# Reciprocal roots of mean squares: one power operation on GpSimd in place of ten VectorE operations

## The chip, the cores and the metric

The kernel runs on one core of one Trainium2 chip. The metric is the device time of one execution in microseconds (us); the kernel before has a median of 2822.03 us over three runs, from 2821.3 to 2822.34. The engines are named as in the profile: PE is TensorE (matmuls and transposes; PEld its weight loads), DVE is VectorE, ACT is ScalarE, POOL is GpSimd, SP is SyncE, which issues nearly all DMAs.

## What is computed

One inference step of a two-layer decoder trunk for 1024 prompt tokens (with 16 meta tokens ahead of them) and 8 sequences of 8 sampled tokens. Layer 0 is a Mamba-2 mixer and a SwiGLU feed-forward; its output gives one shared K and V; layer 1 is sliding-window attention over them and a second feed-forward; a final norm ends it. Every norm divides by the root of a mean square:

```python
def _rmsnorm(x, g):
    xf = x.astype(jnp.float32)
    r = lax.rsqrt(jnp.mean(xf * xf, axis=-1, keepdims=True) + EPS)
    return (xf * r).astype(x.dtype) * g

def _gated_group_rmsnorm(y, z, g):
    u = (y * jax.nn.silu(z)).astype(jnp.float32).reshape(b, l, SSM_GROUPS, D_INNER // SSM_GROUPS)
    u = u * lax.rsqrt(jnp.mean(u * u, axis=-1, keepdims=True) + EPS)
    return u.reshape(b, l, D_INNER).astype(y.dtype) * g
```

Only `lax.rsqrt` is touched: one number for each token and norm (for each token and group in the gated norm).

## The kernel before

The tokens are worked on in two halves, of 592 and 512 (`HALVES`), and each half in blocks of up to 128 tokens. Activations stand with features on the 128 partitions and tokens along the free axis, as residual tiles `hA`, `big` or `hN`. A large product is a row of matmuls by 128 x 128 blocks of weights, three for each block: value and weight are split into a high and a low part (`uH`, `uL`, `wH`, `wL`), and three of the four products are taken (lines 75 to 77 and 1555 to 1557).

The mean squares of a block are columns: one number for each token, tokens on the partitions, and one column for each block of the half. So the function `rsqrt` (line 85) always works on a tile of 128 partitions and 1 to 5 columns. It is called 21 times, from four places:

- `input_half` (line 382), five times. ACT squares the rows of a block and sums them into `xv` (line 379), line 381 divides and adds EPS, and line 401 multiplies the rows by the root into `xn`. PE transposes `xn` (line 406), and ACT and DVE split the result into `uH` and `uL` (lines 81 and 82). Three calls stand at the start of the program, two near 500 us, while the mixer of the first half still runs.
- `norm` (line 820), eight times: the gated norm of each of four groups in each half. PE sums the squares with a column of ones (line 818), line 819 writes `gv`, line 824 puts the roots on a diagonal, PE spreads it over the partitions with a matmul (line 829), and line 832 multiplies. POOL sets `gv` to one first (line 816).
- `row_scale` (line 1145), six times: the norms ahead of the feed-forwards and of K, V and the queries. `col_scale` (lines 1158 and 1159) spreads the root in the same way, or ACT multiplies by it when it reads a product (line 2035).
- `Final.scale` (line 1825), twice. `turn` transposes the result on PE (line 1835) and multiplies by the root into `Y` (line 1843), which is written out.

The ten operations take the root by a shift and subtraction on the bits and two steps of refinement. Each reads what the one ahead of it wrote.

Other names that the text below uses: `gate_tile` (lines 776 and 777) makes the gate `zT` from an accumulator in PSUM by a tanh on ACT and an operation on DVE; `apply_gate` (line 783) multiplies it into `xT`, ACT squares the result (lines 786 and 789), and POOL adds up the squares (line 790). `Weights` loads weights (line 116), casts the high part on ACT (line 152) and takes the low part `wL` on DVE and on POOL in turn (line 158). `gb` is the gain of the first norm, loaded in line 358.

The order on each engine is not written by hand: the program is handed to a scheduler, which orders every engine's instructions by a timeline that it works out when the kernel is built. Each engine then runs its list in order, and an instruction that waits holds up all behind it on its engine.

Of the kernel before, what the change touches and what calls it, by code (L numbers as in the profile page):

```python
# [11 lines left out]
F32 = mybir.dt.float32  # L12
F32R = mybir.dt.float32r
I32 = mybir.dt.int32
AF = mybir.ActivationFunctionType
ALU = mybir.AluOpType
# [68 lines left out]
def rsqrt(nc, pool, v, n, tag):  # L85

    p = v.shape[0]
    si = pool.tile([128, n], I32, name="rs_i", tag="rs_i")
    y = pool.tile([128, n], F32, name=tag + "_y", tag=tag + "_y")
    t = pool.tile([128, n], F32, name="rs_t", tag="rs_t")  # L90
    nc.vector.tensor_scalar(si[:p], v.bitcast(I32), 1, None, ALU.logical_shift_right)
    nc.vector.tensor_scalar(si[:p], si[:p], -1, 0x5F3759DF, ALU.mult, ALU.add)
    nc.vector.tensor_tensor(t[:p], si[:p].bitcast(F32), si[:p].bitcast(F32), ALU.mult)
    nc.vector.scalar_tensor_tensor(t[:p], t[:p], -0.5, v, ALU.mult, ALU.mult)
    nc.vector.scalar_tensor_tensor(y[:p], t[:p], 1.5, si[:p].bitcast(F32), ALU.add, ALU.mult)
    nc.vector.tensor_tensor(t[:p], y[:p], y[:p], ALU.mult)
    nc.vector.tensor_tensor(t[:p], t[:p], v, ALU.mult)
    nc.vector.tensor_scalar(y[:p], y[:p], 0.375, None, ALU.mult)
    nc.vector.scalar_tensor_tensor(t[:p], t[:p], -10.0 / 3.0, t[:p], ALU.add, ALU.mult)
    nc.vector.scalar_tensor_tensor(y[:p], t[:p], 5.0, y[:p], ALU.add, ALU.mult)  # L100
    return y


# [168 lines left out]
class Mamba:  # L272
# [61 lines left out]
    def input_half(self, hf):  # L334
# [35 lines left out]
        for cs in groups:  # L370
# [9 lines left out]
            w = v[:nr, : len(cs)]  # L380
            nc.vector.tensor_scalar(w, w, 1.0 / D, EPS, ALU.mult, ALU.add)
            r = rsqrt(nc, self.wk, w, len(cs), f"rx{cs[0]}")
            self.rtok += [r[:, i : i + 1] for i in range(len(cs))]
            if hf:
# [425 lines left out]
    def norm(self, G, g):  # L810
# [6 lines left out]
        for c, (o, m) in enumerate(H["blocks"]):  # L817
            nc.tensor.matmul(ps[:m, 2 * c : 2 * c + 1], G.ssq[:, o : o + m], K.ones[:, 0:1], start=True, stop=True)
            nc.vector.tensor_scalar(v[:m, c : c + 1], ps[:m, 2 * c : 2 * c + 1], 0.25 / 512, EPS, ALU.mult, ALU.add)
        r = rsqrt(nc, self.wk, v[:, :nb], nb, "rg")  # L820

        dg = lambda o, m: G.ssq[:m, o : o + m]
# [305 lines left out]
def row_scale(K, blocks, pool, ps, apart=None):  # L1128


    nc = K.nc
    nb = len(blocks)
    v = pool.tile([128, nb], F32, name="rv", tag=f"rv{nb}")
    nc.gpsimd.memset(v[:], 1.0)
    for i, (o, n) in enumerate(blocks):
        parts = [K.tot[:, o : o + n]] + ([] if apart is None else [apart[:, o - blocks[0][0] : o - blocks[0][0] + n]])
        for x, src in enumerate(parts):
            nc.tensor.matmul(ps[:n, 2 * i : 2 * i + 1], src, K.ones[:, 0:1], start=x == 0, stop=x == len(parts) - 1)
    pv = ps[:, : 2 * nb].rearrange("p (i two) -> p i two", two=2)[:, :, 0]
    f = 0 if blocks[0][1] == 128 else 1  # L1140
    if f:
        n0 = blocks[0][1]
        nc.vector.tensor_scalar(v[:n0, 0:1], pv[:n0, 0:1], 1.0 / D, EPS, ALU.mult, ALU.add)
    nc.vector.tensor_scalar(v[:, f:], pv[:, f:], 1.0 / D, EPS, ALU.mult, ALU.add)
    return rsqrt(nc, pool, v[:], nb, f"rr{nb}")
# [1468 lines left out]
```

## Time and profile before

| | |
|---|---|
| median of three runs | 2822.03 us |
| span of the profiled execution | 2818.3 us |
| median less span | 3.7 us |
| PE idle in the span | 82.2 us |
| mean granted clock of PE | 0.992 |
| operations in the function, all calls | 210 on DVE |

The profile gives the profiled execution by its span, from the first instruction to the last; the 3.7 us beside it are what the median of the runs has around that. In rows of the timeline the first column is the start in us from the beginning of the span and the second the duration in us, and square brackets give the idle time of that engine just ahead of the row and what ended it. In rows of groups the number behind "x" counts instructions, the next ones are busy us and mean ns of one, and behind the second bar stands the idle time ahead of them. In rows of waits stand the waiting engine, tile and line, whom it waited for, the us in total, the times, and the longest. Rows of windows give, for a stretch, its length, the busy us of PE, PEld, DVE, ACT and POOL with counts, the granted clock of PE (1.00 is full), the DMA share and GB/s.

### The profile page before, as it was taken

To read this page: it belongs to the slowest core of one execution; us is meant where nothing else is said; L and a number is where in the kernel's file an instruction comes from. 1 tells how busy PE (TensorE), PEld (TensorE's weight loads), DVE (VectorE), ACT (ScalarE), POOL (GpSimd) and SP (SyncE) were. 2 spreads that over 40 slices of the span, in tenths; PEclk is the share of its full clock that TensorE was granted. 3 is DMA by queue.
4 is the path that set the end of the run, shared out by engine and by line. 5 is a ranking of instruction groups with operands and counts; after the bars stand their busy time and mean duration, and the time that the engine had idled before them with its cause. 6 is when DMAs were issued, how large, how long until landed. Compare 5 with 4: busy or idle time off the path is not lost. (4 is left out here: it accounts for less than half of the span.)

```text
span 2818.3 us, 51270 instructions
## 1 busy us (share of the span) xinstructions
PE 2736.1 (97%) x19990; PEld 2536.6 (90%) x19990; DVE 2023.9 (72%) x3649; ACT 1230.4 (44%) x2596; POOL 495.8 (18%) x692
## 2 busy tenths in 40 slices
PE   7999999899999899999999999999999999999998
PEld 7988999887888799999999997766999999999998
DVE  6779676647665698777779792455489777777886
ACT  4777554346542344333343233456344333434224
POOL 2566444314223100000000002343210000000000
PEclk9999999999999999999999999999999999999999
DMA  6776767465554524444468663001814443438754
GB/s 206 251 226 226 262 225 241 163 233 199 200 184 155 168 77 166 150 142 138 154 223 326 241 221 98 23 25 41 223 60 144 159 141 130 158 141 289 272 210 159
DMA packets 328289, 496.58 MB, mean 176 GB/s; under 512 B 24607, under 2 KB 222687, under 8 KB 328017
## 3 DMA queue, kind: packets, MB, share of 16 engines
q1 hardware_dynamic: 324590, 486.74, 51.3%
q10 hardware_dynamic: 3456, 6.56, 0.6%
q8 instruction: 158, 2.59, 0.4%
q14 instruction: 85, 0.70, 0.1%
HBM read 317.93 MB, written 175.30 MB: 175 GB/s over the span
## 5 line engine op out<-in xcount | busy, mean ns | idle before, releaser
L1211 ACT CAST wo<-ws 128x512 fp32r<-128x512 f32 x428 | 263.9, 620 | 531.5 <-PE wacc L1556 240.3
L1555 PE MATMUL dacc<-bo,wo 128*128 128x276 f32 (+1 forms) x1232 | 357.7, 291 | 3.7 <-DVE hN L1584 1.4
L1556 PE MATMUL dacc<-bo,wo 128*128 128x276 f32 (+1 forms) x1232 | 355.6, 289 | 0.0
L1557 PE MATMUL dacc<-bo,wo 128*128 128x276 f32 (+1 forms) x1232 | 355.5, 289 | 0.0
L1212 DVE TENSOR_TENSOR wo<-ws,wo 128x512 fp32r<-128x512 f32 x428 | 296.8, 698 | 52.3 <-ACT wo L1211 43.7
L75 PE MATMUL acc<-uH,wH 128*128 128x296 f32 (+1 forms) x840 | 277.6, 331 | 1.8 <-DVE th L777 1.0
L77 PE MATMUL acc<-uH,wL 128*128 128x296 f32 (+1 forms) x840 | 277.0, 330 | 0.4 <-POOL wL L158 0.4
L76 PE MATMUL acc<-uL,wH 128*128 128x296 f32 (+1 forms) x840 | 276.0, 329 | 0.0
L1555 PEld LDWEIGHTS dacc<-bo,wo 128*128 128x128 f32 x1232 | 231.9, 188 | 4.9 <-ACT sumX L1743 1.9
L1556 PEld LDWEIGHTS dacc<-bo,wo 128*128 128x128 f32 x1232 | 231.8, 188 | 0.0
L1557 PEld LDWEIGHTS dacc<-bo,wo 128*128 128x128 f32 x1232 | 231.7, 188 | 0.0
L75 PEld LDWEIGHTS acc<-uH,wH 128*128 128x128 f32 x840 | 159.5, 190 | 17.3 <-issue 6.3
L76 PEld LDWEIGHTS acc<-uL,wH 128*128 128x128 f32 x840 | 159.4, 190 | 12.4 <-issue 4.1
L77 PEld LDWEIGHTS acc<-uH,wL 128*128 128x128 f32 x840 | 159.4, 190 | 11.3 <-issue 2.2
L600 DVE SCALAR_TENSOR_TENSOR cc<-raw,convw,cc 128x616 f32<-128x616 f32 (+1 forms) x144 | 137.5, 958 | 38.7 <-ACT cc L598 36.8
L75 PE MATMUL acc<-yH,wH 128*128 128x296 f32 (+1 forms) x360 | 121.9, 339 | 9.8 <-DVE zT L777 5.9
L2408 POOL MEMSET mask<- 128x64 f32 x1 | 0.2, 151 | 720.3 <-PE dacc L1557 720.3
L77 PE MATMUL acc<-yH,wL 128*128 128x296 f32 (+1 forms) x360 | 119.7, 333 | 1.2 <-DMA wL<-kept 1.2
L76 PE MATMUL acc<-yL,wH 128*128 128x296 f32 (+1 forms) x360 | 120.0, 333 | 0.0
L1731 DVE TENSOR_TENSOR hN<-hN,dacc 128x552 f32<-128x552 f32 (+1 forms) x132 | 94.7, 723 | 20.7 <-PE dacc L1557 20.1
L1555 PE MATMUL wacc<-N4H,wo 128*128 128x276 f32 (+1 forms) x352 | 102.8, 292 | 4.4 <-DVE hA L1568 2.4
L1211 ACT CAST wo<-sum 128x512 fp32r<-128x512 f32 x62 | 38.5, 621 | 155.3 <-PE wacc L1556 107.2
(605 smaller groups left out, 8631.0 us busy)
## 6 DMA issues: line engine op xcount, KB each, us to landing
kept<-wH SPq DMA_DIRECT2D x56, 512.0 KB
kept<-wL SPq DMA_DIRECT2D x56, 512.0 KB
ws<-ffn_w_gate SPq DMA_DIRECT2D x44, 512.0 KB
ws<-ffn_w_up SPq DMA_DIRECT2D x44, 512.0 KB
ws<-ffn_w_down SPq DMA_DIRECT2D x44, 512.0 KB
ws<-ssm_w_in SPq DMA_DIRECT2D x40, 512.0 KB
wH<-kept SPq DMA_DIRECT2D x38, 512.0 KB
wL<-kept SPq DMA_DIRECT2D x38, 512.0 KB
```

The costliest lines, as they stand in the source:

```text
L75: nc.tensor.matmul(out, wH, xH, start=start, stop=False)
L76: nc.tensor.matmul(out, wH, xL, start=False, stop=False)
L77: nc.tensor.matmul(out, wL, xH, start=False, stop=stop)
L600: nc.vector.scalar_tensor_tensor(o, raw[:, k : k + n], w(k), o, ALU.mult, ALU.add)
L1211: nc.scalar.copy(H, src)
L1212: (low or nc.vector).tensor_tensor(L, src, H.bitcast(F32), ALU.subtract)
L1555: nc.tensor.matmul(out, wH, xH, start=start, stop=False, skip_group_check=True)
L1556: nc.tensor.matmul(out, wH, xL, start=False, stop=False, skip_group_check=True)
L1557: nc.tensor.matmul(out, wL, xH, start=False, stop=stop, skip_group_check=True)
L1731: add = lambda d, s: nc.vector.tensor_tensor(d, d, s, ALU.add)
L2408: nc.gpsimd.memset(A.mask0[:, :NS], NEG)
```

## The change

`rsqrt` fills a tile of up to five columns with -0.5 on POOL and raises the mean squares to that power in one two-input POOL operation. The ten DVE operations and the tiles `rs_i` and `rs_t` go.

```diff
 def rsqrt(nc, pool, v, n, tag):
 
     p = v.shape[0]
-    si = pool.tile([128, n], I32, name="rs_i", tag="rs_i")
+    e = pool.tile([128, 5], F32, name="rs_e", tag="rs_e")
     y = pool.tile([128, n], F32, name=tag + "_y", tag=tag + "_y")
-    t = pool.tile([128, n], F32, name="rs_t", tag="rs_t")
-    nc.vector.tensor_scalar(si[:p], v.bitcast(I32), 1, None, ALU.logical_shift_right)
-    nc.vector.tensor_scalar(si[:p], si[:p], -1, 0x5F3759DF, ALU.mult, ALU.add)
-    nc.vector.tensor_tensor(t[:p], si[:p].bitcast(F32), si[:p].bitcast(F32), ALU.mult)
-    nc.vector.scalar_tensor_tensor(t[:p], t[:p], -0.5, v, ALU.mult, ALU.mult)
-    nc.vector.scalar_tensor_tensor(y[:p], t[:p], 1.5, si[:p].bitcast(F32), ALU.add, ALU.mult)
-    nc.vector.tensor_tensor(t[:p], y[:p], y[:p], ALU.mult)
-    nc.vector.tensor_tensor(t[:p], t[:p], v, ALU.mult)
-    nc.vector.tensor_scalar(y[:p], y[:p], 0.375, None, ALU.mult)
-    nc.vector.scalar_tensor_tensor(t[:p], t[:p], -10.0 / 3.0, t[:p], ALU.add, ALU.mult)
-    nc.vector.scalar_tensor_tensor(y[:p], t[:p], 5.0, y[:p], ALU.add, ALU.mult)
+    nc.gpsimd.memset(e[:, :n], -0.5)
+    nc.gpsimd.tensor_tensor(y[:p], v, e[:p, :n], ALU.pow)
     return y
```

Behind the function every line number is smaller by nine in the changed kernel: 392 there is 401 before, 774 is 783, 768 is 777, 372 is 381. Since the scheduler orders the whole program anew, rows move at other places too, on all engines, most of them between 32 and 490 us.

At the start of the program, POOL's list in the changed kernel, from the first row behind its memsets to the first low parts of weights (`rx_y` is the root, `xv` the mean square, `rs_e` the tile of -0.5):

```order
L91 ISA
L91 TENSOR_TENSOR rx_y<-xv,rs_e 80x1
L90 MEMSET rs_e 128x2
L91 TENSOR_TENSOR rx_y<-xv,rs_e 128x2
L90 MEMSET rs_e 128x5
L91 TENSOR_TENSOR rx_y<-xv,rs_e 128x2
L90 MEMSET rs_e 128x5
L149 TENSOR_TENSOR wL<-ws,wH 128x512 x2
```

Before, the row `ISA` and the two rows of `wL` followed each other with nothing between; now three powers, each waiting for a mean square of DVE, stand ahead of these `wL`.

DVE's list at the second call of the start, before (the copy to `hA` moves transposed rows out of PSUM):

```order
L381 TENSOR_SCALAR xv<-xv 128x2
L91 TENSOR_SCALAR rs_i<-xv 128x2
L82 TENSOR_TENSOR uL_94<-ps,uH_92 128x4x80
L92 TENSOR_SCALAR rs_i<-rs_i 128x2
L82 TENSOR_TENSOR uL_95<-ps,uH_93 128x4x80
L93 TENSOR_TENSOR rs_t<-rs_i 128x2
L396 COPY hA<-ps 128x4x128
L94 SCALAR_TENSOR_TENSOR rs_t<-rs_t,xv 128x2
```

and in the changed kernel:

```order
L82 TENSOR_TENSOR uL_94<-ps,uH_92 128x4x80
L387 COPY hA<-ps 128x4x128
L372 TENSOR_SCALAR xv<-xv 128x2
L82 TENSOR_TENSOR uL_95<-ps,uH_93 128x4x80
L392 SCALAR_TENSOR_TENSOR xn<-xr,rx_y,gb 128x512 x2
L392 SCALAR_TENSOR_TENSOR xn<-tot,rx_y,gb 128x512 x2
L372 TENSOR_SCALAR xv<-xv 128x2
L149 TENSOR_TENSOR wL<-ws,wH 128x1024
```

The copy has moved ahead of the mean square, and the rows of `xn` follow with one other operation between.

DVE's list near 493 us, at the first call for the second half, before:

```order
L92 TENSOR_SCALAR rs_i<-rs_i 128x2
L783 TENSOR_TENSOR xT<-xT,zT 128x592 x3
L93 TENSOR_TENSOR rs_t<-rs_i 128x2
L94 SCALAR_TENSOR_TENSOR rs_t<-rs_t,xv 128x2
L95 SCALAR_TENSOR_TENSOR rx_y<-rs_t,rs_i 128x2
L96 TENSOR_TENSOR rs_t<-rx_y 128x2
L97 TENSOR_TENSOR rs_t<-rs_t,xv 128x2
L98 TENSOR_SCALAR rx_y<-rx_y 128x2
L99 SCALAR_TENSOR_TENSOR rs_t<-rs_t 128x2
L100 SCALAR_TENSOR_TENSOR rx_y<-rs_t,rx_y 128x2
L401 SCALAR_TENSOR_TENSOR xn<-xr,rx_y,gb 128x512 x4
L777 SCALAR_TENSOR_TENSOR zT<-zT,acc 128x592
```

and in the changed kernel:

```order
L688 TENSOR_TENSOR S<-S,ps 128x512
L372 TENSOR_SCALAR xv<-xv 128x2
L774 TENSOR_TENSOR xT<-xT,zT 128x592 x3
L392 SCALAR_TENSOR_TENSOR xn<-xr,rx_y,gb 128x512 x4
L768 SCALAR_TENSOR_TENSOR zT<-zT,acc 128x592
L843 TENSOR_TENSOR hA<-hA,acc 128x592
```

The eight rows of the function behind `xT` and the two ahead of it are gone, and `xn` stands right behind `xT`; the order of the others is the same. On POOL the power of this call stands between the rows `xT<-xT,tot` and `sq<-sq,th`.

## The prediction

> **What bounds the kernel now.** I read the page's head first, then the waits of TensorE, then the two stretches in which those waits lie.
>
> ```profile
> span 2818.3 us, 51270 instructions
> PE 2736.1 (97%) x19990; PEld 2536.6 (90%) x19990; DVE 2023.9 (72%) x3649; ACT 1230.4 (44%) x2596; POOL 495.8 (18%) x692
> ```
>
> TensorE (PE) is busy for 2736.1 of 2818.3 us. The matmuls stay, so a change off TensorE can win back at most the 82.2 us in which it is idle, plus what slow restarts cost. The span is that of the profiled execution; the median of the three runs, 2822.0 us, lies 3.7 us above it, and I apply every difference to that median.
>
> The waits of PE, and the row of one removed line:
>
> ```profile
> PE ps L406 <- DVE xn L401: 8.7, 3, 3.7
> PE acc L75 <- DVE zT L777: 6.6, 2, 5.9
> L92 DVE TENSOR_SCALAR rs_i<-rs_i x21: 149/171/536, 6.9 to 2806.2; 128x5 int32<-128x5 int32 x10, 128x4 int32<-128x4 int32 x6, 128x2 int32<-128x2 int32 x4, 80x1 int32<-80x1 int32 x1
> ```
>
> There are 21 calls of the function. Ten operations each at a median of about 0.17 us make 210 x 0.17 = 36 us of VectorE (DVE) work. Its engine is idle for 28% of the span, so this sum says nothing yet: what counts is where a result of the function ends a wait of PE. I followed all 21 calls; PE waits behind six of them: the three at the start, one at 499 us, one at 937 and the last.
>
> **The price of the new operation.** No row shows a power on GpSimd (POOL). The nearest rows and the hop between the engines:
>
> ```profile
> L1872 POOL TENSOR_TENSOR rt<-kr,rope_sb 128x32 f32<-128x32 f32 (+1 forms) x36 | 8.1, 256 | 35.6 <-ACT kr L2035 35.6
> 31.73 0.22 DVE L237 COPY gains<-ps 128x64 f32<-128x64 f32 x1 [1.10 <-PE ps L235]
> 32.04 0.62 POOL L1021 TENSOR_TENSOR wdt<-wdt,gains 128x256 f32<-128x256 f32 x1 [8.35 <-DVE gains L237]
> ```
>
> From below, a power takes no less than the shortest two-input POOL row, 0.26 us. From above, ten such operations for the ten steps give 2.6 us. That is no hard end, since a routine inside the engine may do more than ten steps; longer ones are a rival below. I take **d = 0.8 us**, the middle of 0.26 and 2.6 by ratio. The hop from DVE to POOL is 32.04 - 31.95 = 0.1 us, and I take the same back. A link from the mean square to its first reader then takes d + 0.2 = 1.0 us. The constant's memset is issued ahead of time and costs 0.1 us of an idle POOL.
>
> **The tail: 0.8 us.**
>
> ```profile
> 2805.99 0.17 DVE L91 TENSOR_SCALAR rs_i<-rv 128x5 int32<-128x5 int32 x1
> 2807.81 2.05 DVE L1843 TENSOR_SCALAR Y<-dacc,fr_y 128x512 f32<-128x512 f32 x3
> 2808.61 1.76 PE L1835 MATMUL dacc<-cmask_sb,hN 128*128 128x128 f32 x8 [1.88 <-DVE Y L1843]
> ```
>
> Here the chain is bare: PE waits for Y, Y for the root. The link is 2807.81 - 2805.99 = 1.82 us now and 1.0 after, and nothing else lies beside it until the end.
>
> **The last gated norm: 0.85 us.**
>
> ```profile
> 935.03 0.17 DVE L91 TENSOR_SCALAR rs_i<-gv 128x4 int32<-128x4 int32 x1
> 936.89 0.87 DVE L824 TENSOR_SCALAR sq<-cmask_sb,rg_y 128x128 f32<-128x128 f32 x4
> 937.23 0.49 PE L829 MATMUL acc<-sq,cmask_sb 128*128 128x128 f32 x2 [1.53 <-DVE sq L824]
> ```
>
> The link is 936.89 - 935.03 = 1.86 us now. It shrinks by about 0.85, less than the 1.53 us in which PE waits.
>
> **The start: 1.5 us.** All of the first 31 us feed the first large matmul.
>
> ```profile
> 6.70 0.15 DVE L91 TENSOR_SCALAR rs_i<-xv 80x1 int32<-80x1 int32 x1
> 9.54 1.41 DVE L401 SCALAR_TENSOR_TENSOR xn<-xr,rx_y,gb 80x512 f32<-80x512 f32 x2 [1.18 <-DMA gb<-ssm_norm_g]
> 13.53 0.49 DVE L82 TENSOR_TENSOR uL<-ps,uH 128x320 fp32r<-128x320 f32 x1
> 14.00 0.69 DVE L396 COPY hA<-ps 128x512 f32<-128x512 f32 x1
> 15.87 1.42 DVE L401 SCALAR_TENSOR_TENSOR xn<-xr,rx_y,gb 128x512 f32<-128x512 f32 x2
> 18.61 3.57 POOL L158 TENSOR_TENSOR wL<-ws,wH 128x512 fp32r<-128x512 f32 x2 [17.61 <-ACT wH L152]
> 19.73 1.23 DVE L93 TENSOR_TENSOR rs_t<-rs_i 128x2 f32<-128x2 f32 x1
> 25.62 2.74 DVE L401 SCALAR_TENSOR_TENSOR xn<-S,rx_y,gb 128x512 f32<-128x512 f32 x4
> 31.63 0.40 PE L75 MATMUL acc<-uH,wH 128*128 128x296 f32 x1
> ```
>
> The first call wins nothing: its reader waits for the DMA of gb until 9.54. In the second, the new DVE order puts the copy L396 where the second L82 now stands, so that it ends at 13.53 + 0.69 = 14.2, and the mean square behind it; 0.17 us for the square and a link of 1.0 let xn start at 15.4 instead of 15.87: 0.5 us. For the third, nine more small steps leave DVE between 15.7 and 25.6. Eight of them take 0.07 us (where they overlap) to 0.17 us each, and L93 takes 1.23: 1.8 to 2.6 us. Against that, xn of this group moves up beside POOL's two L158, and each may hold up one xn for 1.25 us: 2.5 us. The bounds are -0.2 and 3.1; I take the middle.
>
> **The wait at 499 us: 1.1 us, or 7.3.** This is the largest single wait behind a root.
>
> ```profile
> 493.16 0.43 DVE L381 TENSOR_SCALAR xv<-xv 128x2 f32<-128x2 f32 x1
> 493.90 2.14 DVE L783 TENSOR_TENSOR xT<-xT,zT 128x592 f32<-128x592 f32 x3
> 496.23 1.47 POOL L790 TENSOR_TENSOR sq<-sq,th 128x592 f32<-128x592 f32 x1 [2.67 <-ACT th L789]
> 496.34 1.38 DVE L95 SCALAR_TENSOR_TENSOR rx_y<-rs_t,rs_i 128x2 f32<-128x2 f32 x1
> 497.65 2.52 POOL L158 TENSOR_TENSOR wL<-ws,wH 128x512 fp32r<-128x512 f32 x2
> 497.75 1.21 DVE L96 TENSOR_TENSOR rs_t<-rx_y 128x2 f32<-128x2 f32 x1
> 501.61 0.16 DVE L100 SCALAR_TENSOR_TENSOR rx_y<-rs_t,rx_y 128x2 f32<-128x2 f32 x1
> 501.81 2.74 DVE L401 SCALAR_TENSOR_TENSOR xn<-xr,rx_y,gb 128x512 f32<-128x512 f32 x4
> 504.46 0.76 DVE L777 SCALAR_TENSOR_TENSOR zT<-zT,acc 128x592 f32<-128x592 f32 x1
> 505.28 0.61 PE L75 MATMUL acc<-yH,wH 128*128 128x296 f32 x1 [5.88 <-DVE zT L777]
> ```
>
> PE waits from 499.40 until L777 has read its accumulator. Steps on two columns, 0.16 us elsewhere, take 1.2 to 1.4 us here: L95 lasts as long as POOL's L790, and L96 ends with the first half of POOL's L158. So a DVE operation with two SBUF operands sits out the POOL operation under way. The engines take turns, and the function loses about 5 us to that.
>
> ```profile
> 505.28:508.20 2.92, 2.92 (x12) 2.92 (x13) 1.31 (x2) 0.70 (x1) 0.74 (x1) 0.50 0.00 0
> 511.00:514.00 3.00, 3.00 (x24) 3.00 (x23) 1.71 (x2) 0.66 (x2) 0.00 (x0) 1.00 0.58 238
> ```
>
> After the wait 12 matmuls take 2.92 us at a granted clock of 0.50, where 12 take 1.5 at 1.00: 1.4 us more. If xn ran undisturbed, xT would end at 495.8, xn at 498.6 and L777 at 499.3: the whole wait and the slow restart would go, 5.9 + 1.4 = 7.3 us. But xn has two SBUF operands as well, and it now moves beside the POOL work from which it was clear at 501.81. Taking turns with 0.71 us per xT, 0.8 for the power, 0.69 per xn, 1.47 for L790 and 1.26 for each half of L158: the power runs between two xT, xT ends at 496.6, three POOL operations slip between four xn, and L777 starts at 496.6 + 4 x 0.69 + 1.47 + 2 x 1.26 = 503.3 instead of 504.46. I take 1.1 us, by the rows of L95 and L96.
>
> The Trainium skill's GPSIMD Engine Reference, section Key points, says that POOL shares its SBUF interfaces with VectorE, in contention with instructions that have two SBUF inputs. The trace agrees by the 1.21 us of L96 against 0.16. By that rule the sum keeps 1.1 at this place; without it, it takes 7.3.
>
> **What hides the rest.** In both feed-forward norms PE reaches the reader by its own order, later than the root is there:
>
> ```profile
> 981.65 0.87 DVE L1158 TENSOR_SCALAR tot<-cmask_sb,rr_y 128x128 f32<-128x128 f32 x4
> 985.97 1.05 PE L1159 MATMUL ps<-tot,cmask_sb 128*128 128x128 f32 x8
> 2088.90 1.01 DVE L1158 TENSOR_SCALAR tot<-cmask_sb,rr_y 32x32 f32<-32x32 f32 x5
> ```
>
> At 981.65 + 0.87 the factor is ready 3.5 us ahead of PE; at 2088.90 it is ready 2 us ahead. A link that is 0.8 us shorter wins nothing there, and one 2 us longer costs nothing. The other calls have PE busy behind them as well. A wait of POOL in its own order is hardly new:
>
> ```profile
> L816 POOL MEMSET gv<- 128x8 f32 x8 | 0.8, 104 | 25.1 <-DVE rs_t L97 25.1
> ```
>
> This memset stands on POOL near the new power and now waits 25.1 us in all for step L97 of the function; the power waits for the earlier mean square. Queued behind it are the copies of raw and the product L737.
>
> **Sum**: 0.8 + 0.85 + 1.5 + 1.1 = 4.25 us, so 2822.0 - 4.25 = **2817.8 us**.
>
> The same page, section Engine selection, advises VectorE for elementwise work and gives GpSimd as 1.96 times slower. An estimate by that figure, twice the 0.17 us of a DVE step, makes a power of 0.33 us, and the sum about 6 us. No run here shows it for a power.
>
> **The rivals.**
> 1. *The mid wait goes wholly*: xn runs ahead of POOL. For it: DVE issues the four xn back to back. Against it: L95 to L99 each met a POOL operation. Price: 6.2 us more, 2811.6 us.
> 2. *The power is long.* Each microsecond of d adds one at the tail, at 937, at 499 and about one at the start, so the gain is gone at d = 0.8 + 4.25/4 = 1.9 us, and from 3.3 us the kernel is slower than a measurement can miss. For it: one operation does ten steps' work and more. Against it: the tiles have at most 5 columns. At d = 5: tail and 937 +3.4 each; the start +5 (first root at 6.7 + 5.2 = 11.9, past the 9.54 of gb, and the second behind it on POOL); 499 +3; 2088.9 overruns its 2 us by 1.4. That is 16 us: 2838.
> 3. *Another order.* The scheduler moves other work too between 32 and 490 us:
>
> ```profile
> 32.00:490.00 458.00, 446.53 (x3531) 412.95 (x3530) 332.79 (x526) 276.47 (x660) 231.67 (x268) 0.99 0.71 233
> ```
>
> PE is idle there for 458 - 446.5 = 11.5 us. That may double or halve: 2829 or 2812. I see no sign either way.
> 4. *POOL cannot start early.* Its first two-input operation in the trace is at 18.61; the new one is due at 6.8, and its cover ends at 9.54. Up to 18.6 + 0.8 + 0.1 - 9.5 = 10 us, if it is not ready before; the middle gives 2823. POOL has been idle since 1.0, which speaks against it. The same page, section Instruction dispatch, states about 6 us for the first call of a loaded kernel; from 1.0 that ends at 7 us, within the cover.
>
> **Chances.** Forecast 0.42, the mid wait gone 0.18, a long power 0.20, another order 0.14, a late start 0.06. A difference of 0.2%, 5.6 us, is about what a measurement of this kernel can tell from none. Below 2816.4 lie the second case, a third of the first and some of the order: 0.36. Above 2827.7 lie most of the long powers and some of the order: 0.24. The rest, 0.40, is no difference. The lower end takes every gain at its bound (3.1 + 7.3 + 1.4 + 1.4 at d = 0.26): 2808.8. At d = 2.6 the sum is 3 us of loss; the upper end is set at 2832, so that only the longer powers stay out. The forecast's own range is 2814 to 2822.
>
> **What would show it.** The power's row on POOL gives d. At the tail, the time from the last mean square to Y should be 1.0 us. At 935 PE's wait for L824 should be near 0.7. At 499 PE's wait for zT should be near 4.8 us with xn stretched beyond 0.75 each; if it is gone, the turns are wrong. The first large matmul should start near 30.1 instead of 31.63. The forecast is wrong if d is over 1.9 us, or if PE's waits between 32 and 490 us sum to much else than 11.5.

## The result, and the profile after

The changed kernel takes **2807.43 us** (median of 4 runs, 2804.66 to 2810.73); the kernel before took 2821.91 us in the same session (4 runs, 2821.3 to 2822.34). The ratio is **0.9946, 95% interval 0.9933 to 0.9960**: 14.5 us less, where 4.25 us were forecast. A later session gave 0.9939 (0.9927 to 0.9950). The profiled execution of the changed kernel took 2804.66 us, at the fast end of its four.

The head of the page, the main waits of TensorE and the power's groups (minimum, median and maximum in ns; first and last start in us):

```profile
span 2802.9 us, 51082 instructions
PE 2734.6 (98%) x19990; PEld 2536.4 (90%) x19990; DVE 1993.7 (71%) x3439; ACT 1229.3 (44%) x2596; POOL 518.6 (19%) x734
PE ps L397 <- DVE xn L392: 5.3, 3, 3.3
PE acc L75 <- DVE zT L768: 3.8, 2, 3.0
L91 POOL TENSOR_TENSOR rg_y<-gv,rs_e x8: 1004/1098/1575, 213.2 to 927.3; 128x5 f32<-128x5 f32 x4, 128x4 f32<-128x4 f32 x4
L91 POOL TENSOR_TENSOR rx_y<-xv,rs_e x5: 548/711/1603, 6.8 to 520.6; 128x2 f32<-128x2 f32 x4, 80x1 f32<-80x1 f32 x1
L91 POOL TENSOR_TENSOR fr_y<-rv,rs_e x2: 1167/1168/1168, 2767.9 to 2791.2; 128x5 f32<-128x5 f32 x2
```

PE's idle time falls from 82.2 to 68.3 us; its busy time falls by 1.5. So in this pair of profiles nearly the whole gain is waits that went. A power takes 0.55 us on one column, 0.71 on two and 1.0 to 1.2 on four or five, and up to 1.6 us where DVE works beside it.

The two bare links, at the last gated norm and in the tail, in the timeline:

```profile
927.32 1.02 POOL L91 TENSOR_TENSOR rg_y<-gv,rs_e 128x4 f32<-128x4 f32 x1 [15.66 <-DVE gv L810]
928.71 0.49 PE L820 MATMUL acc<-sq,cmask_sb 128*128 128x128 f32 x2 [0.77 <-DVE sq L815]
2790.88 0.14 DVE L1815 TENSOR_SCALAR rv<-dacc 32x1 f32<-32x1 f32 x1
2791.16 1.17 POOL L91 TENSOR_TENSOR fr_y<-rv,rs_e 128x5 f32<-128x5 f32 x1 [21.97 <-DVE rv L1815]
2792.36 2.06 DVE L1834 TENSOR_SCALAR Y<-dacc,fr_y 128x512 f32<-128x512 f32 x3 [1.35 <-POOL fr_y L91]
```

PE's wait at the gated norm is 0.77 us instead of 1.53. In the tail DVE waits 1.35 us for the root; the steps there took 1.82 us.

The place that was the wait of 5.88 us at 505 us:

```profile
489.54 0.43 DVE L372 TENSOR_SCALAR xv<-xv 128x2 f32<-128x2 f32 x1
489.98 2.15 DVE L774 TENSOR_TENSOR xT<-xT,zT 128x592 f32<-128x592 f32 x3
490.05 1.27 POOL L91 TENSOR_TENSOR rx_y<-xv,rs_e 128x2 f32<-128x2 f32 x1
492.05 6.01 DVE L392 SCALAR_TENSOR_TENSOR xn<-xr,rx_y,gb 128x512 f32<-128x512 f32 x4
492.32 1.82 POOL L781 TENSOR_TENSOR sq<-sq,th 128x592 f32<-128x592 f32 x1 [0.84 <-ACT th L780]
494.09 3.41 POOL L149 TENSOR_TENSOR wL<-ws,wH 128x512 fp32r<-128x512 f32 x2
497.98 0.76 DVE L768 SCALAR_TENSOR_TENSOR zT<-zT,acc 128x592 f32<-128x592 f32 x1
498.79 0.62 PE L75 MATMUL acc<-yH,wH 128*128 128x296 f32 x1 [3.00 <-DVE zT L768]
```

Four `xn` that took 2.74 us before now take 6.01, 1.5 us each, beside three POOL operations, and PE still waits 3.00 us. The turns came, as forecast; the wait shrank by 2.9 us all the same.

### Where the time went

All profiles hold 19990 matmuls, so the start of the n-th can be compared between them. (At 262 us the n-th is not the same operation in every kernel, since the scheduler moves rows there: that cut is rough.) The table cuts the program at matmuls 263, 1854, 3612, 3862, 5997, 6513, 18091 and the last, counted from 0; the times are those of the first profile of the kernel before. Each entry is how much longer a stretch took than in that profile, averaged over profiles of kernels "without" the power in the calls that count for the stretch (the first profile itself as 0) and "with" it:

- Up to 490 us the three calls of the start decide: without are both profiles of the kernel before, `e2_rg`, `e3_rr`, `e6_late` and `e9_b_one`; with are both of the changed kernel, `e1_rx`, `e4_dead`, `e5_start` and `e10_a_one`.
- From 490 to 534 us the two late calls decide: without are both of the kernel before, `e2_rg`, `e3_rr` and `e5_start`; with are both of the changed kernel, `e1_rx` and `e6_late` (`e4_dead`, left out here, has -1.6).
- Behind 534 us, without are both of the kernel before, `e1_rx`, `e5_start`, `e6_late` and `e9_b_one`; with are both of the changed kernel, `e4_dead` and `e10_a_one`.

| stretch, us | forecast | without (profiles) | with (profiles) | difference |
|---|---|---|---|---|
| 0 to 52, the start | -1.5 | 0.15 (6) | -2.06 (6) | -2.2 |
| 52 to 262 | 0 | -0.10 (6) | -2.76 (6) | -2.7, rough |
| 262 to 490 | 0 | 0.45 (6) | 0.65 (6) | 0.2, rough |
| 490 to 534 | -1.1 | -0.32 (5) | -4.80 (4) | **-4.5** |
| 534 to 927 | 0 | 0.05 (6) | 0.24 (4) | 0.2 |
| 927 to 1026 | -0.85 | -2.40 (6) | -4.75 (4) | -2.3, not firm |
| 1026 to 2570 | 0 | 2.6 (6) | 1.4 (4) | not told apart |
| 2570 to the end | -0.8 | 0.15 (6) | -1.98 (4) | -2.1 |

"Half clock" below means stretches of 3.4 us or a multiple in which PE's granted clock is 0.50; each 3.4 us in which PE is busy costs 1.7.

The stretch from 1026 to 2570 us tells nothing of the change: its entries lie between 0 and 6.0 without and between -1.2 and 4.9 with. Between 927 and 1026 us the entries without run from 0 to -5.4 (`e1_rx`), past every entry with. There only the wait at the last gated norm follows its own call: it is some 0.77 us in all profiles with one power in that call and 1.53 in those with the ten steps. The first profile of the kernel before was slower than most between 927 and 1026 us, by 2.4 on average, and faster than most behind it.

Near 308 us (matmul 2194) all these kernels have done the same matmuls again. From 52 us to there the entries are -0.1 on average without (-1.8 to 0.6) and -1.9 with (-3.1 to -0.9), a difference of 1.7 us.

### The profile page after: what moved, and what is told of

Its sections match the earlier page's. It is cut to its first block, busy times and chain, and to the rows that moved or that the text cites. A ratio compares the mean times of both kernels' runs of the same rounds, so it can differ in the third digit from the quotient of the medians.

```text
span 2802.9 us, 51082 instructions
## 1 busy us (share of the span) xinstructions
PE 2734.6 (98%) x19990; PEld 2536.4 (90%) x19990; DVE 1993.7 (71%) x3439; ACT 1229.3 (44%) x2596; POOL 518.6 (19%) x734
```

## The experiments

Ratios are to the kernel before in the same session, whose median there was 2821.3 to 2824.1 us; a ratio of 0.001 is 2.8 us.

| kernel | ratio | 95% interval |
|---|---|---|
| the change, again (`e8_after`) | 0.9939 | 0.9927 to 0.9950 |
| power in the five rx calls (`e1_rx`) | 0.9957 | 0.9945 to 0.9969 |
| power in the eight rg calls (`e2_rg`) | 0.9994 | 0.9985 to 1.0002 |
| power in rr and fr (`e3_rr`) | 0.9994 | 0.9985 to 1.0003 |
| power, and the ten steps as well (`e4_dead`) | 0.9936 | 0.9924 to 0.9948 |
| power in the three calls of the start (`e5_start`) | 0.9969 | 0.9958 to 0.9981 |
| power in the two calls at 490 and 521 us (`e6_late`) | 0.9984 | 0.9975 to 0.9992 |
| the kernel before, again (`e7_before`) | 0.9996 | 0.9985 to 1.0006 |
| before, one split moved (`e9_b_one`) | 0.9980 | 0.9968 to 0.9993 |
| the change, one split moved (`e10_a_one`) | 0.9963 | 0.9950 to 0.9975 |
| the change, all splits on DVE (`e11_a_dve`) | 0.9982 | 0.9971 to 0.9993 |
| five steps, no power (`e12_five`) | 0.9980 | 0.9969 to 0.9990 |
| before, two splits moved (`e13_b_two`) | 0.9993 | 0.9983 to 1.0003 |
| each power twice (`e14_twice`) | 0.9971 | 0.9961 to 0.9981 |

### Which calls: three parts, and the load alone

The parts choose by the tag of the call; everything else is the kernel before:

```diff
+    if tag[:2] in ('rx',):
+        p = v.shape[0]
+        e = pool.tile([128, 5], F32, name="rs_e", tag="rs_e")
+        y = pool.tile([128, n], F32, name=tag + "_y", tag=tag + "_y")
+        nc.gpsimd.memset(e[:, :n], -0.5)
+        nc.gpsimd.tensor_tensor(y[:p], v, e[:p, :n], ALU.pow)
+        return y
```

with `('rg',)` and `('rr', 'fr')` in the second and third. In the fourth the power gives the result, and the ten operations stay on DVE with a tile of their own that nothing reads.

> The power only in the five calls of the input half's norms (rx, 7 to 521 us); the other sixteen calls keep their ten VectorE operations. Theory A, waits add up (each call shortens the waits of TensorE behind its own chain): the start keeps its 0.9 us and the wait at 499 us gives its 2.9 us, so 4 to 5 us under the kernel before, and the waits at 937 us (1.53) and in the tail (1.88) stay as they were. Theory B, relief (VectorE has 210 operations less, and work far from a call comes sooner): 5 of 21 calls, so about a quarter of 14.5 us, 3 to 4 us, spread over the places from 52 to 540 us. Theory C, a new draw of the order and of the half-clock stretches: any number between 5 us under and 5 us over, with half-clock stretches at other times than in either kernel.

> The power only in the eight gated norms (rg, 213 to 927 us). Theory A: the waits near those calls go as in the changed kernel: 0.8 us at 937 us, some 2 us between 131 and 387 us, some 1.4 us by 534 us, so 4 to 6 us under the kernel before, with the start and the 499 us wait (5.88 us) as before. Theory B: 8 of 21 calls, about 5.5 us, spread from 213 us on. Theory C: anything from 5 us under to 5 us over; the sum of the three partial kernels then need not be the 14.5 us of the whole.

> The power only in the six row scales (rr, 832 to 2075 us) and the two final norms (fr). Theory A: the tail's 0.6 us, and the 2 to 4 us that the changed kernel won between 955 and 1030 us if they belong to these calls, so 1 to 5 us under the kernel before; nothing before 830 us. Theory B: 8 of 21 calls, about 5.5 us, all after 830 us. Theory C: the 4.8 us between 937 and 1030 us were a draw of half-clock stretches and do not come back with these calls alone; within 2 us of the kernel before or to either side of it.

> All 21 results come from the power, but VectorE still does the ten operations of each call into a tile that nobody reads, and the scheduler is free to put them behind urgent work. So the link is short and VectorE's load is that of before. Theory A (short link): nearly the whole gain stays, 11 to 15 us under the kernel before. Theory B (relief of VectorE): the 7 to 8 us that came far from the links go again, 5 to 7 us under. Theory C: between 0 and 15 us under, with half-clock stretches elsewhere, and the waits that do not come back at the same places in the two kernels decide it.

The five rx calls carry most: 12 us of 2823, with 1.7 us each for the other two groups, neither of which can be told from none. The three ratios lack 0.0055 together, and the whole change 0.0054 to 0.0061: the parts add up. Theory A holds in that, but its prices do not: for rx, 4 to 5 us, it was too small, and for rg, 4 to 6 us, too large. Theory B's 5.5 us for each of the two other groups lie outside their intervals, which end at 4.2 us.

The fourth run decides against relief of DVE. The head of its page:

```profile
PE 2733.7 (97%) x19990; PEld 2533.9 (90%) x19990; DVE 2021.6 (72%) x3649; ACT 1228.6 (44%) x2596; POOL 520.2 (19%) x734
```

DVE is as busy as before (2023.9 us), with all 210 operations back, and the gain is whole. At one place the load is seen: the wait at 499 us is 4.91 us there instead of 3.00, since one of the dead steps stands ahead of `zT`. The total does not show it.

### Start and late calls apart, and both kernels again

```diff
+    if tag in ("rx1", "rx3") or (tag == "rx0" and n == 1):
```

and, for the late two,

```diff
+    if tag == "rx2" or (tag == "rx0" and n == 2):
```

> The power only in the first three norms of the input (rx of the first half, 7 to 18 us); the other eighteen calls keep ten VectorE operations. Theory A (each call's own chain): the matmul at 490 us comes 3.5 to 4 us sooner than in the kernel before, as in the run with all five rx calls (4.0), of which 2 us are won in the start and 2 us by 262 us; the waits at 505 us (5.88) and 534 us (1.05) stay; 4 us in all, with or without the 3 to 5 us that every kernel so far gained between 927 and 1030 us. Theory D (a shift in time lets VectorE and GpSimd meet at other places, and that makes the gain by 262 us): the start keeps under 2.5 us by 52 us and the rest comes at the decx waits (2.42 and 2.05 us) by a VectorE operation that no longer stands beside GpSimd's weight split. Theory C: the total anywhere within 6 us of the kernel before.

> The power only in the two norms of the second half's input (rx, 490 and 521 us). Theory A: nothing before 490 us; the 5.88 us wait falls to about 3.0 and the 1.05 us wait at 534 us goes, so 4.0 to 4.5 us under the kernel before by 534 us. Theory C: the wait falls as said, but half-clock stretches put 1.7 us steps on either side. The step between 927 and 1030 us: if it comes here as well (3 to 5 us), where nothing was edited after 521 us, it belongs to no call.

> The kernel before, unchanged, for a second profile of it. If the 3 to 5 us between 927 and 1030 us are a draw of one execution, this profile may lie several us ahead of the first one by 1030 us, with the first kernel's waits at 955, 972 and 976 us (1.51, 1.41 and 1.03) smaller; if they are lasting, its matmuls stand within 1 us of the first profile's everywhere up to 1030 us. The ratio of times is 1.000 within its interval either way.

> The changed kernel, unchanged, in the same call as the parts: its ratio says whether the run with the ten operations added (0.9936) is the same as the change (0.9946) or better. Theory A and the falling of theory B: 0.993 to 0.996, the same as the run with the dead operations within the interval; the start and late parts and the two small groups add up to it.

The start alone gives 8.8 us (5.4 to 11.9), the late two 4.5 us (2.3 to 7.1); together about as much as the rx calls at once. In the start's profile the matmul at 490 us comes 7.2 us sooner, where theory A had 3.5 to 4. Of these, 4.6 come by 52 us: PE is idle 2.7 us less, and the rest is half-clock time less in that execution. A further 1.9 us come between 52 and 308 us, with the calls themselves far behind. PE's two waits for `decx` there, 2.42 us at 193 us and 2.05 at 280 in the kernel before, are 0.43 and 1.48; they are the place that theory D named. Part of what they give goes again: PE now waits 1.32 us for a DMA (`big<-state_ssm`) at 201 us and 0.94 us at 212, where the kernel before has no wait between 195 and 250 us.

The late calls bring the 5.88 us wait to 2.99 and 5.5 us by 534 us: 3.9 us less idle time of PE, and the rest half-clock time. The second profile of the kernel before stays within 1 us of the first at every cut up to 927 us and is 2.2 us ahead at 1026 us, with waits of 0.84 and 0.61 us at `big` where the first had 1.41 and 1.03. So part of the gain that a single pair of profiles shows there was the first profile's own.

### What the waits were made of: moving GpSimd's splits, without any power

`SHARE` says which low parts of weights go to POOL (1) and which to DVE (0). The first kernel moves one of POOL's 28 splits, the second two others, both in the kernel before; the third does the first edit in the changed kernel, the fourth moves all:

```diff
-SHARE = (1, 0)
+SHARE = (1, 0) * 25 + (0, 0) + (1, 0) * 6
```

```diff
+SHARE = (1, 0) * 9 + (0, 0) + (1, 0) * 3 + (0, 0) + (1, 0) * 18
```

```diff
+SHARE = (0,)
```

> The kernel before, with ten VectorE operations in every call, and one edit elsewhere: of the 28 weight splits that GpSimd does (two halves each), the one that stands beside the chain of ten at 497 us goes to VectorE as one operation. Theory of turns (what made the wait of 5.88 us was four of the ten small operations, each sitting out a half split, 1.2 to 1.4 us in place of 0.16): the small operations fall back to 0.16 us, some 4.5 us go, VectorE takes a split of about 1.25 us in, and the wait falls to between 2 and 4 us; 2 to 4 us faster by 534 us without any power operation. Rival (the chain's ten operations and its order made the wait): the wait stays at 5 us or more, and the time is that of the kernel before.

> The kernel before, with ten VectorE operations in every call, and the two of GpSimd's weight splits that stand beside the decx operations at 190 and 277 us put on VectorE. Theory of turns (the 2.42 and 2.05 us waits for decx are small VectorE operations sitting out GpSimd's splits; the changed kernel merely re-timed them): decx operations of 0.3 us in place of 3.42 and 5.11 for four, both waits fall under 1.2 us, and 1.5 to 3 us are gained by 290 us without any power. Rival (decx waits for the order on VectorE or for ScalarE): both waits stay at 2 us, and VectorE's own split of 1.25 us makes them longer.

> The changed kernel with the same single split moved from GpSimd to VectorE. Theory of turns: the four operations that took 6.01 us beside GpSimd take 3.0 to 4.5, the wait of 3.00 us falls to between 0.5 and 2, and the kernel is 1 to 2 us under the changed one, about 0.9930. Rival (the 3.00 us are the xn operations' place ahead of the gate, whatever GpSimd does): the wait stays at 3 us, and the time is that of the changed kernel, 0.994.

> The changed kernel with all 28 of GpSimd's weight splits on VectorE (28 x 1.28 us in place of 56 x 1.39 us on GpSimd). Theory of turns: 78 us of GpSimd's work that VectorE must sit out is replaced by 36 us of its own, so the waits behind VectorE shrink further, the decx waits among them, and the kernel is 2 to 6 us under the changed one. Rival (VectorE at 71% has no room: the splits' own lateness holds TensorE): waits on the split weights grow, and the kernel is 0 to 10 us over the changed one.

With the split gone from beside the steps, in the kernel before (`e9_b_one`):

```profile
498.52 1.46 POOL L790 TENSOR_TENSOR sq<-sq,th 128x592 f32<-128x592 f32 x1 [2.66 <-ACT th L789]
498.64 1.37 DVE L95 SCALAR_TENSOR_TENSOR rx_y<-rs_t,rs_i 128x2 f32<-128x2 f32 x1
500.04 0.16 DVE L96 TENSOR_TENSOR rs_t<-rx_y 128x2 f32<-128x2 f32 x1
500.24 0.17 DVE L97 TENSOR_TENSOR rs_t<-rs_t,xv 128x2 f32<-128x2 f32 x1
504.00 0.37 PE L75 MATMUL acc<-yH,wH 128*128 128x296 f32 x1 [2.31 <-DVE zT L777]
```

L95 still meets POOL's L790 and takes 1.37 us; L96 and L97, which took 1.21 and 1.19 us beside the split, take 0.16 and 0.17. PE's wait falls from 5.88 to 2.31 us, more than the power brought, and the kernel gains 5.6 us (2.0 to 9.0). But only a part of the fall is turns. From the start of L95 to the operation behind L100 DVE takes 503.10 - 498.64 = 4.5 us, with the moved split among it, instead of 501.81 - 496.34 = 5.5. The larger part, some 2.7 us, is order: `zT` now stands ahead of the four `xn` (2.74 us) and not behind them. The wait came out as the theory of turns had it, but the larger part of the reason did not.

The same at 190 us. DVE's rows of `decx` and PE's waits for it, first in the kernel before, then with two splits moved (`e13_b_two`), then in the changed kernel:

```profile
PE ps L750 <- DVE decx L716: 4.5, 2, 2.4
189.83 3.42 DVE L716 TENSOR_TENSOR decx<-xw,decx 32x128 fp32r<-32x128 f32 x1
```

```profile
191.56 0.98 DVE L716 TENSOR_TENSOR decx<-xw,decx 32x128 fp32r<-32x128 f32 x3
191.99 0.78 PE L750 MATMUL ps<-decB,decx 96*128 96x512 f32 x2 [1.18 <-DVE decx L716]
```

```profile
PE ps L741 <- DVE decx L707: 1.9, 2, 1.5
186.99 1.85 DVE L707 TENSOR_TENSOR decx<-xw,decx 32x128 fp32r<-32x128 f32 x2 [0.95 <-ACT decx L705]
```

One operation of 3.42 us stood beside POOL's L790 and split; three take 0.98 us without them. PE's waits of 2.42 and 2.05 us for `decx` fall to 1.18 us and to nothing. But the split on DVE takes 3.25 us beside POOL, other waits of 1.2 and 1.6 us appear, and the time is not told from that of before: in its profile nothing is won between 52 and 308 us (0.3 us more than in the first profile), where the theory had 1.5 to 3 us by 290. In the changed kernel, and in every kernel with the power in the start, with POOL's splits as they were, the scheduler puts the first `decx` ahead of the split instead of beside it, and the waits are 0.45 and 1.49 us. In all profiles with the ten steps in the start, and no split moved near it, the first of these waits is 2.4 us; in all but one of them (`e2_rg`) 3.4 us at half clock follow it, and in none with the power in the start.

In the changed kernel the moved split (`e10_a_one`) won nothing, and the theory of turns missed: the four `xn` still take 5.16 us beside POOL's other operations, and the wait is 3.37 us, because DVE now does the split (1.21 us) ahead of `zT`. The ratio is worse than the change's. In the one profile most of that lies between 1343 and 2080 us, where nothing was edited and which has 6.8 us more of half clock than the changed kernel's; the mean clocks of its five runs, 0.989 to 0.991 against 0.990 to 0.995 in the nine of the changed kernel, fit that. Why they are lower was not settled.

With all splits on DVE (`e11_a_dve`) the wait is 5.82 us, so DVE's own queue is the limit at that place, as the rival had it. But of the 10 to 12 us by which this kernel is slower than the changed one, 8 to 10 lie between 1026 and 2570 us in its profile, most of them at half clock, so the total does not decide for the rival.

### Shorter steps, and a longer power

The first kernel leaves out the second refinement, so its roots are less exact; in the second the power is issued twice:

```diff
-    nc.vector.tensor_tensor(t[:p], y[:p], y[:p], ALU.mult)
...
-    nc.vector.scalar_tensor_tensor(y[:p], t[:p], 5.0, y[:p], ALU.add, ALU.mult)
```

```diff
+    nc.gpsimd.tensor_tensor(y[:p], v, e[:p, :n], ALU.pow)
```

> No power: every call on VectorE with the first five of the ten operations; the second refinement of the root is left out. Theory A (it is the length of the chain that counts, on whatever engine): half of the chain's length gives part of the gain of every place: 0.8 us or more in the start, the same new order of work with its smaller waits between 180 and 290 us, the 5.88 us wait at 3 to 4.5, the tail's 1.88 at about 1.1; 6 to 12 us under the kernel before. Rival (the power's own engine matters, because the chain no longer stands on VectorE): under 4 us.

> Each of the 21 calls runs the power twice into the same tile, so each link is 0.55 to 1.17 us longer and GpSimd works about 21 us more. Theory A (each call counts where its own chain ends last): 0.55 to 0.7 us at the start's second link, about 0.5 at 499 us, 1.0 at 929 us, 1.2 in the tail, nothing elsewhere: 3 to 4 us over the changed kernel, 0.995 to 0.996. Rival (the change's gain lies in the new order that came with it): the order stays nearly as it is and the time is within 2 us of the changed kernel, or the order is drawn again and 5 us or more go.

Five steps give 5.6 us (2.8 to 8.7), a little under what theory A allowed; the tail's wait is 1.08 us, as expected. The wait at 193 us stays at 2.41 us and that at 499 at 5.01: half the chain does not bring the new order, and the steps left still take turns. So in the rx calls half the length on DVE is not enough.

The doubled power gives back 7 to 9 us of the gain, twice what was expected. Its profile at the last gated norm and in the tail:

```profile
928.96 0.49 PE L821 MATMUL acc<-sq,cmask_sb 128*128 128x128 f32 x2 [1.86 <-DVE sq L816]
2799.41 1.97 PE L1827 MATMUL dacc<-cmask_sb,hN 128*128 128x128 f32 x8 [2.62 <-DVE Y L1835]
```

There the second power costs what it lasts, 1.1 and 1.3 us, as expected; at 499 us it costs 0.65. The start shows nothing of the 0.55 to 0.7 us expected there. Most of the rest lies between 927 and 1026 us, where four further waits are each longer by 0.3 to 1.0 us than in the changed kernel (among them `big`, 1.34 us for 0.37, and `hA`, 2.43 for 1.83) and 1.4 us more go at half clock. Why these waits take the one value or the other was not settled.

## Why the prediction was wrong

At the places that the forecast named, its mechanism was right: shorter links, and turns with POOL. By the table and the two bare links these places gave some 8 of the 14.5 us (2.2 in the start, 4.5 from 490 to 534 us, 0.8 at the last gated norm, 0.5 in the tail), where the sum had 4.25. The rest lies where the sum had nothing: 1.7 us between 52 and 308 us, up to 1.5 us of waits behind the last gated norm, which are not firm, and 1.7 to 2.0 us of another pace at the end; what is left is not told from the scatter. The measured 2807.4 us lie 1.4 us below the lower end of the range, 2808.8 us. That end took each call at its bound; neither another order nor a wait away from the calls was in it.

**The wait at 499 us**, put at 1.1 us, is the step whose working failed, by 3.4 us for the stretch. From the mean square to `zT` the kernel before has 504.46 - 493.16 = 11.3 us and the prediction 503.3 - 493.16 = 10.1; the changed kernel takes 497.98 - 489.54 = 8.4. Of these last 1.7 us, 0.9 are the three `xT`: I let the power push between them, but they took 2.15 us as before, and the power was the one that was held up (1.27 us instead of 0.71). The other 0.8 us are the four `xn` with their three POOL operations: 6.75 us by my count, one strictly after the other, and 5.93 in the trace. So the wait fell by 2.9 us. The call at 521 us, counted with those that have PE busy behind them, gave some 0.8 us more: PE's wait of 1.05 us for `hA` went, and the next, for `xT`, grew from 0.58 to 0.84. Together PE's idle time in the stretch is 3.9 us shorter in each of the four profiles with the power; most of the other 0.6 us is half-clock time. `e6_late` shows the stretch alone.

The Trainium skill's GPSIMD Engine Reference, section Key points, on which the lower value leaned, states that there is contention, not that it must cost the one engine as much as the other. The steps agree with it: L96 takes 1.21 us beside a split and 0.16 without one. The three `xT` beside the power show none of it on DVE's side.

**Another order**, given nothing in the sum and 11.5 us of PE's idle time as its stake, was the second step that failed. I saw no sign either way; there was one. PE's first wait for `decx`, 2.42 us, stood on an operation of 0.28 us that took 3.42 beside POOL, and 3.4 us at half clock followed it. With the power in the start that wait is 0.45 us and the half clock behind it is gone. The second wait, 2.05 us at 280 us, on an operation that took 4.10, is 1.49. Between 52 and 308 us the kernels with the power in the start are 1.7 us shorter on average: 0.7 us of it is PE's idle time, since new waits stand where the old ones went, and the rest is half-clock time. One profile without the power in the start, `e2_rg`, is as far ahead (1.8 us): its wait is 2.42 us, but no half clock follows.

The sign that the prediction named, a sum of PE's waits between 32 and 490 us away from 11.5 us, did not come: it is 458 - 447.4 = 10.6 us in the changed kernel. That POOL's splits made the two waits is shown by `e13_b_two`. That they carry the gain is not shown, since that kernel had won nothing by 308 us. That the power in the start is enough for the new order is shown by `e5_start`; why the scheduler then orders so was not settled, and the order itself was not forced by hand.

**The start**, put at 1.5 us, gave 2.2 us; the first large matmul of the profile came at 29.17 us, not 30.1. The second `xn` started at 14.23 us, 1.6 us sooner instead of 0.5. Its link was 14.23 - 13.25 = 1.0 us with the square, 0.2 less than forecast, but the copy ahead of it ended at 13.3 and not 14.2, since the L82 ahead of that ran at 11.20 and not, as before, behind the mean square at 13.06. Some 0.4 us at the first `xn` are the execution's own: `gb` landed sooner. The middle of the bounds was too low.

**The last gated norm** was right: 0.76 us of wait against 0.85, with a longer power (1.02 us) and shorter hops (0.1 us together). The stretch up to 1026 us holds 2.3 us; what goes beyond this wait are further waits behind it, which I had set at nothing. They do not follow the calls: PE's wait for `big` near 955 us is 0.37 us in the changed kernel but 1.46 in `e4_dead`, which has every power, and it is missing in `e1_rx`, which has the ten steps there.

**The tail** was too high: the link is 1.34 us instead of 1.0, because a power on five columns takes 1.17 us and not 0.8; 0.5 us were won. The stretch from 2570 us shows 2.1 us, and most of it is a pace that no step of mine had (below).

**The price of the power** was too low for four and five columns and right for two. The break-even of 1.9 us was nowhere near. The Trainium skill's GPSIMD Engine Reference advises VectorE in its section Engine selection, and gives the factor of 1.96 in its section Elementwise — side-by-side cycle accounting, for an add on large tiles; the estimate by it was 0.33 us. The rows of 0.55 to 1.2 us speak against using that factor for a power.

**A late start of POOL** did not come: the first power ran at 6.78 us, 0.15 us behind its mean square, with no delay that a row shows. **What hides the rest** held for the feed-forward norms: PE has no wait for their factors (L1150) in the changed kernel, and `e3_rr` alone is not told from no change. It did not hold for the call at 521 us.

No version here beats the changed kernel by more than the intervals.

## What to carry to other kernels

When a small chain sits beside another engine's large operations, ask first how much of its time is its own: here 0.16 us steps took 1.2 to 1.4 us, and moving one neighbour, with the order that came of it, won as much there as removing the chain. When a scheduler orders everything anew, look for waits that are already badly placed in the stretch behind the edit; they bound what a new draw can give from the gain's side. A wait that goes is worth only what the next ones leave: with two splits moved, 2.4 and 2.1 us of waits fell to 1.2 and nothing, and no time was won. And a gain of half a per cent is to be read from several profiles of both kernels, for a single pair can mislead by 2 us in one stretch and by 6 in another.

## What was not expected of the hardware

**One pace too many.** In the long run of feed-forward matmuls, the same instructions at a granted clock of 1.00 run at two paces. A window of 150 us (length, PE busy with its count, PEld, DVE, ACT, POOL, clock, DMA share, GB/s), first in the kernel before, then in the changed one:

```profile
2600.00:2750.00 150.00, 150.00 (x1197) 150.00 (x1196) 125.71 (x197) 35.62 (x58) 0.00 (x0) 1.00 0.69 241
```

```profile
2587.00:2737.00 150.00, 150.00 (x1207) 150.00 (x1207) 127.84 (x201) 36.55 (x60) 0.00 (x0) 1.00 0.69 243
```

1197 matmuls against 1207, with PE never idle. The second profiles of both kernels show 1197 and 1208, `e6_late` 1197 and `e3_rr` 1208, so it goes with the program rather than with the execution. It does not go with the power as such: `e4_dead`, with every power, shows 1197. In both profiles of the changed kernel it is worth 1.7 to 2.0 us over the whole run. What sets it stays open.

**Half clock.** After some waits the granted clock falls to half. Between 1780 and 2100 us of the time axis, in the kernel before and in the change with all splits on DVE:

```profile
1780.00:2100.00 320.00, 308.38 (x2303) 253.69 (x2302) 190.04 (x627) 159.96 (x507) 100.29 (x145) 0.99 0.29 81
```

```profile
1780.00:2100.00 320.00, 308.08 (x2229) 253.78 (x2228) 182.51 (x577) 155.88 (x486) 103.05 (x147) 0.96 0.28 80
```

PE is busy for the same 308 us, at a mean clock of 0.96 instead of 0.99: some 10 us of the 320. The stretch from 1343 to 2080 us took up to 11 us more in some profiles than in the first one, most of it half-clock time (in `e3_rr`, 5.9 of 10.1 us are longer waits). The runs of the kernel before scatter by about as much, from 2817 to 2830 us at mean clocks of 0.994 to 0.988, and on the whole the longer ones have the lower clock.
